# Splitting FFN weights in the DMA queue instead of on VectorE, with four more block steps

## Chip, core and metric

The kernel runs on one core of a Trainium2 chip. The metric is the device time of one execution in microseconds, median over the runs; lower is better. Engine names are those of the profile: PE is the TensorE matmul array, PEld its weight load, DVE is VectorE, ACT is ScalarE, POOL is GpSimd, SP is SyncE, which here only issues DMAs.

## What is computed

The reference is a backbone of two layers over 512 latent tokens of 1024 channels, all in float32. Layer 0 has two attention groups, layer 1 a Fourier mixing; both end in a gated convolutional feed-forward block (FFN). The FFN is the part that the change touches:

```
def conv_ffn(h, w_up, conv_w, conv_b, w_down):
    u = h @ w_up                                   # 512 x 1024 @ 1024 x 5632
    up = jnp.pad(u, ((0, 0), (1, 1), (0, 0)))
    u = up[:, :-2] * conv_w[0] + up[:, 1:-1] * conv_w[1] + up[:, 2:] * conv_w[2] + conv_b
    gate, val = jnp.split(u, 2, axis=-1)
    return (jax.nn.silu(gate) * val) @ w_down      # 512 x 2816 @ 2816 x 1024
```

## The kernel before

**A product of three.** PE multiplies in float32r, which keeps fewer bits than float32. So each operand is kept as a pair: a rounded high part h and the rest l = x - h. A product is then three matmuls (function `mm3`): L97 takes the high part of the weights with the high part of the activations, L98 the high part of the weights with the low part of the activations, L99 the low part of the weights with the high part of the activations. In the rows below the weight is called `wh` or `wl`.

**The split.** A weight comes by one DMA from SP into a buffer `raw` (three of them, `raw()` at L127 to L130). `split` at L119 then makes the pair: ACT copies `raw` into `wh` (that rounds), DVE subtracts `wh` from `raw` into `wl`. Pairs lie in five slots of 128 x 1024 elements each (`wpair`, L132: tag "wh" with 5 buffers and tag "wl" with 5). A slot is taken again once the last matmul that reads it is done.

**The FFN.** The 2816 inner channels are 22 steps of 128, fi = 0 to 21. A step multiplies h by the gate and the value columns of `w_up` (1 MB of weights), puts the result through the convolution (ACT, DVE), gates it and splits it for the down product. The steps are done in three groups of 8, 6 and 8 (`GROUPS`); after each group come eight down products, d = 0 to 7, each with its own weights `w_down` (512 KB, in the middle group 384 KB). Steps 0 to 2 run ahead in another form and are not touched.

**Plain and block steps.** A plain step has two pairs of 128 x 1024 and 2 x 8 x 3 = 48 matmuls of 128x512. A block step (`seven_products`) cuts the product into 2 x 2 blocks and does seven products instead of eight, in the order 1, 5, 2, 6, 4, 3, 7, each 4 x 3 = 12 matmuls of 128x256, 84 in all. Its weights are four pairs (`seven_weights`): "1" and "24" are blocks of `w_up` as they are; "57" and "63" are sums of blocks that DVE makes first (L986 to L989). Product 1 reads pair "1", products 5 and 7 read "57", products 6 and 3 read "63", products 2 and 4 read "24". The table `SEVEN` names the block steps: 10 in layer 0, 9 in layer 1.

**What sets the order.** Each engine works through its own list in order. The lists are laid out by a scheduler when the program is built; a wait at the head of a list holds all that stands behind it. In layer 0 the FFN also carries `gemv_jobs` (the modulation of layer 1: DMAs of `mod_r`, DVE at L388 and L391), which the program advances a piece at a time (`pump`).

Of the kernel before, what the change touches and what calls it, by code (L numbers as in the profile page):

```python
# [19 lines left out]
P = 128  # L20
# [13 lines left out]

SUMS = [5, 7]

SEVEN = [(5, 6, 8, 10, 12, 14, 15, 17, 18, 20), (8, 9, 11, 12, 14, 15, 17, 18, 20)]
NSKEW = [6, 5]
EPS = 1e-6
SCALE = P ** -0.5  # L40
# [34 lines left out]
def kernel(ctx: ExitStack, tc: tile.TileContext, a):  # L75
# [38 lines left out]
    def held(i):  # L114
        if i.ins.engine in fences:
            tc.add_manual_dep(i.ins, fences[i.ins.engine], mybir.DependencyInfo(
                mybir.DependencyClass.NoSync, mybir.DependencyReason.DATA), reason="fence")

    def split(h, l, src, eng=V):  # L119
        i = S.copy(out=h, in_=src), eng.tensor_tensor(out=l, in0=src, in1=f(h), op=ALU.subtract)  # L120
        for j in i:
            held(j)

    cp = ctx.enter_context(tc.tile_pool(name="cp", bufs=1))
    wp = ctx.enter_context(tc.tile_pool(name="wp", bufs=1))
# [825 lines left out]
    def up_weights(l, pairs, fis, eng=V):  # L951
        for fi in fis:
            r = raw([P, 2, KC, P], a["w_up"][l, fi])
            for i in range(2):
                wh, wl = pairs([P, KC, P])
                split(wh, wl, r[:, i, :, :], eng)
                yield [(wh[:, k, :], wl[:, k, :]) for k in range(KC)]
# [23 lines left out]
    def seven_weights(l, fi):  # L981
        r = raw([P, 2, KC, P], a["w_up"][l, fi])
        s = mk(wp, [P, 4, KH, P], F32, "raw", 3)
        a4 = r.rearrange("p i (c k) n -> p (i c) k n", c=2)

        for j in (V.tensor_tensor(out=s[:, 0:2], in0=a4[:, 3::-3], in1=a4[:, 2].unsqueeze(1).to_broadcast(  # L986
                      [P, 2, KH, P]), op=ALU.add),
                  V.tensor_tensor(out=s[:, 2], in0=s[:, 0], in1=a4[:, 0], op=ALU.add),
                  V.tensor_tensor(out=s[:, 3], in0=s[:, 2], in1=a4[:, 1], op=ALU.add)):  # L989
            held(j)  # L990
        w = {}
        for names, src in (("1", a4[:, 0:1]), ("57", s[:, 0:2]), ("63", s[:, 2:4]), ("24", a4[:, 1::2])):
            wh, wl = wpair([P, len(names), KH, P])
            split(wh, wl, src)
            for i, n in enumerate(names):
                w[n] = wh[:, i], wl[:, i]
        return w
# [59 lines left out]
    def ffn(l, xp, ready, pre, mid, gem, plain=None):  # L1057
# [116 lines left out]
        for gi, (f0, nch) in enumerate(GROUPS):  # L1174
            end = gi == len(GROUPS) - 1
            for fi in range(max(f0, FIRST), f0 + nch):
                if fi == SUMS[l]:
                    bs = seven_inputs(xp)
                if fi in SEVEN[l]:
                    cc = [conv(fi, i, u, None, i == 1) for i, u in enumerate(seven_products(l, fi, pps, bs))]  # L1180
                else:
                    cc = []
                    for i, w in enumerate(up_weights(l, wpair, [fi])):
                        ps = mk(pps, [P, T], F32, "mm", 6)
                        up_mm(ps, w, slice(0, T))
                        cc.append(conv(fi, i, ps))
                gated(fi, cc[0], cc[1], f0)
                if l == 0 and fi not in SEVEN[l]:
                    pump(gem, GP[0])
            g_ = [gs[fi] for fi in range(f0, f0 + nch)]  # L1190
            ws = {}

            def part(d, hs, ps=None):
                ps, sl = y_mm(pps, ws[d], g_, hs, True, ps)
                if gi == 0:
                    S.copy(out=yT[:, d, sl], in_=ps[:, sl])
                else:
                    V.tensor_tensor(out=yT[:, d, sl], in0=yT[:, d, sl], in1=ps[:, sl], op=ALU.add)
                if end:
                    ys.add(pps, yT[:, d, sl], hs)  # L1200

            def weights(d):
                r = raw([P, nch, P], a["w_down%d" % gi][l, d])
                wh, wl = (xp.spare if end and 4 <= d < 7 else wpair)([P, nch, P])
                split(wh, wl, r)
                ws[d] = [(wh[:, c, :], wl[:, c, :]) for c in range(nch)]


            hs = {d: [0, 1] if not end or d == 0 else [0] for d in range(KC)}
            begun = {}  # L1210
            if end:
                pump(gem, 100)
                fence()
            keep = dict(fences)
            fences.clear()
            for d in range(2):
                weights(d)
            fences.update(keep)
            for d in range(2):
                begun[d] = y_mm(pps, ws[d], g_, hs[d], False)[0]  # L1220
            for d in range(KC):
                if d not in ws:
                    weights(d)
                part(d, hs[d], begun.get(d))
                if gem is not None and not end:
                    pump(gem, GP[1])
            if end:
                mid(ys)
                for d in range(1, KC):
                    part(d, [1])  # L1230
# [300 lines left out]
```

## Time and profile before

| | |
|---|---|
| median of 3 runs | 1158.47 us (1157.93 to 1159.31) |
| the profiled execution | 1163.01 us, its span on the core 1161.2 us |
| PE, DVE, ACT, POOL busy | 1119.1, 860.7, 577.2, 169.1 us |
| moved by DMA | 145.31 MB, mean 125 GB/s; the main queue takes 35.1% of the 16 DMA engines' span |
| FFN of layer 0 / layer 1 | about 335 to 685 us / 780 to 1131 us of the span |

A row of the groups reads: line, engine, operation, output<-inputs, shapes, count, then busy us and mean ns of one, then the idle time ahead of them and what ended it. Rows of the timeline have start, duration, engine, line and operation. Matmuls overlap in the pipeline, so the time that one costs is the distance between two starts, not its own duration. In rows of windows the number behind each engine is its busy time in the stretch.

### The profile page before, as it was taken

The numbers are of one execution on the slowest core, as the hardware profiler recorded it, in microseconds if no ns is written. First come the engines' busy times: TensorE is split into PE (matmuls) and PEld (weight loads), VectorE is DVE, ScalarE is ACT, GpSimd is POOL, SyncE is SP. The second block draws the span as 40 slices with busy tenths as digits, with TensorE's granted clock in tenths as the row PEclk, the third lists the DMA queues.
The fourth block names the chain that finished last, engine by engine and source line by source line (L and its number), as shares of the span: only waits on it lengthen the run. The fifth ranks groups of instructions, "written<-read, shape, count | busy, mean of one in ns | idle before, by whom it ended". The sixth has DMA issues, their size and how long they took to land.

```text
span 1161.2 us, 19052 instructions
## 1 busy us (share of the span) xinstructions
PE 1119.1 (96%) x7658; PEld 965.9 (83%) x7658; DVE 860.7 (74%) x1402; ACT 577.2 (50%) x1025; POOL 169.1 (15%) x181
## 2 busy tenths in 40 slices
PE   7999999999999999999899998989999999999995
PEld 4689889669888978887798898869888888899895
DVE  5573776675679966987899658878997497579745
ACT  4342355566665634551465445556843365265442
POOL 1122433212420000000000143430000000000023
PEclk9899999999999999999999999999999999999998
DMA  9532110775202455445524400531217233223212
GB/s 371 201 123 73 37 37 1 290 267 205 74 27 85 146 183 222 175 163 179 189 86 156 145 1 19 185 124 38 73 53 274 73 109 110 76 106 109 91 56 73
DMA packets 29440, 145.31 MB, mean 125 GB/s; under 512 B 2980, under 2 KB 7716, under 8 KB 16424
## 3 DMA queue, kind: packets, MB, share of 16 engines
q1 hardware_dynamic: 29352, 144.09, 35.1%
q8 instruction: 60, 0.98, 0.3%
q14 instruction: 28, 0.23, 0.1%
HBM read 141.98 MB, written 2.10 MB: 124 GB/s over the span
## 4 chain that ended last, share of the span: by engine, by line
PE 80%; DVE 9%; ACT 4%; DMA 3%; issue 1%; POOL 1%; DVEq 0%; SPq 0%; POOLq 0%; ACTq 0%
PE mm L97 22%; PE mm L99 21%; PE mm L98 21%; PE PT L798 2%; PE gm L417 1%; DMA raw<-in_w_up 1%; DVE md_t L288 1%; ACT wh L120 1%; PE O L97 1%; DVE wl L120 1%; PE S L97 1%; PE gm L97 1%; PE O L98 1%; PE gm L98 1%; PE gm L99 1%
## 5 line engine op out<-in xcount | busy, mean ns | idle before, releaser
L120 ACT CAST wh<-raw 128x1024 fp32r<-128x1024 f32 (+2 forms) x189 | 179.9, 965 | 160.1 <-PE mm L98 70.5
L120 DVE TENSOR_TENSOR wl<-raw,wh 128x1024 fp32r<-128x1024 f32 (+3 forms) x177 | 200.4, 1140 | 73.3 <-ACT wh L120 73.1
L97 PE MATMUL mm<-hh,wh 128*128 128x256 f32 (+2 forms) x652 | 220.9, 339 | 2.4 <-ACT wh L120 1.9
L99 PE MATMUL mm<-hh,wl 128*128 128x256 f32 (+2 forms) x652 | 219.0, 336 | 0.2 <-DVE wl L120 0.2
L98 PE MATMUL mm<-hl,wh 128*128 128x256 f32 (+2 forms) x652 | 218.7, 335 | 0.0
L97 PEld LDWEIGHTS mm<-hh,wh 128*128 128x128 f32 x652 | 122.9, 188 | 19.3 <-ACT wh L120 2.3
L99 PEld LDWEIGHTS mm<-hh,wl 128*128 128x128 f32 x652 | 123.1, 189 | 14.9 <-issue 0.4
L263 POOL TENSOR_TENSOR gacc<-gacc,sq 128x256 f32<-128x256 f32 (+1 forms) x35 | 30.2, 864 | 718.4 <-ACT sq L261 717.5
L98 PEld LDWEIGHTS mm<-hl,wh 128*128 128x128 f32 x652 | 123.1, 189 | 13.7
L97 PE MATMUL mm<-xh,wh 128*128 128x512 f32 (+1 forms) x368 | 131.5, 358 | 0.2 <-ACT wh L120 0.2
L98 PE MATMUL mm<-xl,wh 128*128 128x512 f32 (+1 forms) x368 | 130.7, 355 | 0.1
L99 PE MATMUL mm<-xh,wl 128*128 128x512 f32 (+1 forms) x368 | 129.9, 354 | 0.0
L97 PE MATMUL mm<-zh,wh 128*128 128x256 f32 x304 | 87.1, 287 | 1.2 <-ACT wh L120 1.2
L99 PE MATMUL mm<-zh,wl 128*128 128x256 f32 x304 | 84.9, 279 | 0.4 <-DVE wl L120 0.4
L98 PE MATMUL mm<-zl,wh 128*128 128x256 f32 x304 | 84.9, 279 | 0.0
L97 PEld LDWEIGHTS mm<-xh,wh 128*128 128x128 f32 x368 | 69.1, 188 | 13.1 <-issue 1.6
L98 PEld LDWEIGHTS mm<-xl,wh 128*128 128x128 f32 x368 | 69.1, 188 | 11.2 <-DVE xl L120 0.3
L99 PEld LDWEIGHTS mm<-xh,wl 128*128 128x128 f32 x368 | 69.0, 188 | 10.9
L1079 ACT ACTIVATE cv<-mm,cols 128x512 f32<-128x512 f32 x64 | 49.7, 777 | 27.8 <-PE mm L99 21.6
L97 PEld LDWEIGHTS mm<-zh,wh 128*128 128x128 f32 x304 | 57.6, 189 | 5.1 <-ACT sq L1025 2.9
L99 PEld LDWEIGHTS mm<-zh,wl 128*128 128x128 f32 x304 | 57.6, 190 | 0.7 <-DVE wl L120 0.6
L391 DVE SCALAR_TENSOR_TENSOR gacc<-raw,scol,gacc 128x1024 f32<-128x1024 f32 x42 | 53.8, 1282 | 5.8 <-DMA raw<-in_mod_r 5.3
(386 smaller groups left out, 2655.0 us busy)
## 6 DMA issues: line engine op xcount, KB each, us to landing
raw<-in_w_up SPq DMA_DIRECT2D x44, 1024.0 KB, 4.9
raw<-in_mod_r SPq DMA_DIRECT2D x24, 1024.0 KB, 5.0
raw<-in_mod_p SPq DMA_DIRECT2D x16, 1024.0 KB, 4.9
raw<-in_w_down SPq DMA_DIRECT2D x32, 512.0 KB, 3.8
raw<-in_w_in SPq DMA_DIRECT2D x6, 1024.0 KB, 4.8
raw<-in_w_down SPq DMA_DIRECT2D x16, 384.0 KB, 3.1
raw<-in_w_out SPq DMA_DIRECT2D x4, 1024.0 KB, 4.9
raw<-in_w_f SPq DMA_DIRECT2D x8, 512.0 KB, 3.5
```

The lines of the kernel that those rows point to most:

```text
L97: i = PE.matmul(out, lhsT=ah, rhs=bh, start=start, stop=False, skip_group_check=skip)
L98: PE.matmul(out, lhsT=ah, rhs=bl, start=False, stop=False, skip_group_check=skip)
L99: return i, PE.matmul(out, lhsT=al, rhs=bh, start=False, stop=stop, skip_group_check=skip)
L120: i = S.copy(out=h, in_=src), eng.tensor_tensor(out=l, in0=src, in1=f(h), op=ALU.subtract)
L263: G.tensor_tensor(out=self.acc[:, sl], in0=self.acc[:, sl], in1=sq[:, sl], op=ALU.add)
L288: m = V.scalar_tensor_tensor(out=t, in0=yT[:, k, hs], scalar=der[:, l, gi, k:k + 1], in1=R, op0=ALU.mult, op1=ALU.mult)
L391: held(V.scalar_tensor_tensor(out=acc, in0=w[:, i, :], scalar=scol[:, 0, k:k + 1], in1=acc, op0=ALU.mult, op1=ALU.add))
L417: PE.matmul(ps[32 * q:32 * q + 32, :], lhsT=spad[:, k, :], rhs=w[:, q * T:(q + 1) * T], start=k == 0, stop=k == KC - 1)
L798: PE.transpose(out=pt[:, j * P:(j + 1) * P], in_=Ps[j][:, off:off + P], identity=ident)
L1079: S.activation(out=cv, in_=ps, func=AF.Identity, bias=bc, scale=wc[1])
```

## The change

The new helper `split_in` makes a pair without `raw` and without DVE. A DMA from POOL casts the weight from HBM into `wh`; ACT writes -`wh` into `wl`; a second DMA from POOL reads the same weight from HBM again and adds it onto `wl`, which leaves the weight minus its rounded part. Plain steps from fi = 3 on and the down products of the first two groups use it in place of `raw` and `split`. Block steps use it for "1" and "24"; they still load the whole of `w_up` into `raw` by SP for the sums, and "57" and "63" are still split by ACT and DVE. The down products of the last group are as before. `SEVEN` has 12 and 11 steps, 23 instead of 19. The modulation pieces are pumped once or twice in turn per down product. POOL's descriptor ring is twice as large.

```
-SEVEN = [(5, 6, 8, 10, 12, 14, 15, 17, 18, 20), (8, 9, 11, 12, 14, 15, 17, 18, 20)]
+SEVEN = [(5, 6, 8, 9, 10, 12, 14, 15, 16, 18, 19, 20), (8, 9, 10, 11, 12, 14, 15, 16, 18, 19, 20)]
...
+    def split_in(h, l, src):
+        G.dma_start(out=h, in_=src)
+        held(S.activation(out=l, in_=f(h), func=AF.Copy, scale=-1.0))
+        G.dma_start(out=l, in_=src, accum_op=ALU.add)
...
         w = {}
-        for names, src in (("1", a4[:, 0:1]), ("57", s[:, 0:2]), ("63", s[:, 2:4]), ("24", a4[:, 1::2])):
+        for names, src, way in (("1", a["w_up"][l, fi, :, 0:1, :KH], split_in), ("57", s[:, 0:2], split),
+                                ("63", s[:, 2:4], split), ("24", a["w_up"][l, fi, :, :, KH:], split_in)):
             wh, wl = wpair([P, len(names), KH, P])
-            split(wh, wl, src)
+            way(wh, wl, src)
...
                     cc = []
-                    for i, w in enumerate(up_weights(l, wpair, [fi])):
+                    for i in range(2):
+                        wh, wl = wpair([P, KC, P])
+                        split_in(wh, wl, a["w_up"][l, fi, :, i])
                         ps = mk(pps, [P, T], F32, "mm", 6)
-                        up_mm(ps, w, slice(0, T))
+                        up_mm(ps, [(wh[:, k, :], wl[:, k, :]) for k in range(KC)], slice(0, T))
                         cc.append(conv(fi, i, ps))
...
             def weights(d):
-                r = raw([P, nch, P], a["w_down%d" % gi][l, d])
                 wh, wl = (xp.spare if end and 4 <= d < 7 else wpair)([P, nch, P])
-                split(wh, wl, r)
+                src = a["w_down%d" % gi][l, d]
+                if end:
+                    split(wh, wl, raw([P, nch, P], src))
+                else:
+                    split_in(wh, wl, src)
...
-                    pump(gem, GP[1])
+                    pump(gem, GP[1] + d % 2)
...
-    nc = bacc.Bacc("TRN2", target_bir_lowering=False, num_devices=1, dynamic_dma_scratch_size=1024)
+    nc = bacc.Bacc("TRN2", target_bir_lowering=False, num_devices=1, dynamic_dma_scratch_size=2048)
```

In the changed kernel the lines from L120 on stand 6 to 18 lines lower; the two DMAs of `split_in` are L126 (cast) and L128 (add), its ACT copy is L127.

Two places show what the built lists hold. The first is POOL's list at layer 1's first block steps, fi = 8 to 10. Before, POOL has nothing to do in the FFN of layer 1 up to its last group; its list goes from the end of the Fourier stage straight to the sums of squares at the end:

```order
L120 TENSOR_TENSOR wl_1241_8128<-raw_1239_8125,wh_1240_8127 128x1024
L120 TENSOR_TENSOR wl_1243_8132<-raw_1239_8125,wh_1242_8131 128x1024
L263 TENSOR_TENSOR acc_1171_7741<-acc_1171_7741,sq_1208_7967 128x512
L263 TENSOR_TENSOR gacc_1658_11260<-gacc_1658_11260,sq_1659_11266 128x256
L263 TENSOR_TENSOR gacc_1658_11260<-gacc_1658_11260,sq_1664_11301 128x256
```

In the changed kernel there stands between them, among others (128x512 is pair "1", 128x2x512 is pair "24"):

```order
L126 DMA wh_1413_9716<-in_w_up 128x512
L128 DMA wl_1414_9717<-in_w_up 128x512
L126 DMA wh_1419_9729<-in_w_up 128x2x512
L126 DMA wh_1429_9846<-in_w_up 128x512
L128 DMA wl_1420_9730<-in_w_up 128x2x512
L128 DMA wl_1430_9847<-in_w_up 128x512
L126 DMA wh_1435_9859<-in_w_up 128x2x512
L126 DMA wh_1447_9978<-in_w_up 128x512
```

Per block step POOL now issues four DMAs. The cast into `wh_1435` ("24" of step 10) waits for the slot of `wh_1417` ("63" of step 9), that is, for the last matmul of product 3 of step 9; "24" of step 9 (`wh_1419`) waits for product 3 of step 8 in the same way.

The second place is PE's list in the middle of a block step, where pair "24" comes in. Before (step 9; `wh_1437` is "57", `wh_1439` is "63", `wh_1441` is "24"):

```order
L99 MATMUL mm_1443_9618<-zh_1359_9094,wl_1438_9607 128x256
L97 MATMUL mm_1444_9619<-zh_1361_9098,wh_1439_9610 128x256
L98 MATMUL mm_1444_9619<-zl_1362_9099,wh_1439_9610 128x256
L99 MATMUL mm_1444_9619<-zh_1361_9098,wl_1440_9611 128x256
...
L97 MATMUL mm_1443_9618<-hh_5_66,wh_1441_9614 128x256
L98 MATMUL mm_1443_9618<-hl_6_67,wh_1441_9614 128x256
L99 MATMUL mm_1443_9618<-hh_5_66,wl_1442_9615 128x256
```

In the changed kernel (step 9 again; `wh_1415` is "57", `wh_1417` is "63", `wh_1419` is "24"; `wh_1429` and `wh_1431` are "1" and "57" of step 10):

```order
L99 MATMUL mm_1421_9734<-zh_1346_9214,wl_1416_9722 128x256
L97 MATMUL mm_1438_9865<-hh_5_66,wh_1429_9846 128x256
L98 MATMUL mm_1438_9865<-hl_6_67,wh_1429_9846 128x256
L97 MATMUL mm_1437_9864<-zh_1346_9214,wh_1431_9851 128x256
L98 MATMUL mm_1437_9864<-zl_1347_9215,wh_1431_9851 128x256
L97 MATMUL mm_1422_9735<-zh_1348_9218,wh_1417_9725 128x256
...
L97 MATMUL mm_1422_9735<-zh_1350_9222,wh_1419_9729 128x256
L98 MATMUL mm_1422_9735<-zl_1351_9223,wh_1419_9729 128x256
L99 MATMUL mm_1437_9864<-zh_1346_9214,wl_1432_9852 128x256
L99 MATMUL mm_1421_9734<-hh_5_66,wl_1420_9730 128x256
```

Five matmuls of the next step (the four with `wh_1429` and `wh_1431`, and `wl_1432`) now stand inside this one, ahead of the first matmul that reads `wl_1420`. From that matmul to the last one that reads `wh_1417` (the end of product 3, which frees the slot for "24" of step 10) there are 31 matmuls of 128x256, both counted; between them stands no product that doesn't need "24" or come behind it in the list.

## The prediction

> **What bounds the kernel now.** I read the busy times first, then the chain of work that ended last, both on the page.
>
> ```profile
> span 1161.2 us, 19052 instructions
> PE 1119.1 (96%) x7658; PEld 965.9 (83%) x7658; DVE 860.7 (74%) x1402; ACT 577.2 (50%) x1025; POOL 169.1 (15%) x181
> PE 80%; DVE 9%; ACT 4%; DMA 3%; issue 1%; POOL 1%; DVEq 0%; SPq 0%; POOLq 0%; ACTq 0%
> ```
>
> PE sets the time, so an edit is worth what it does to PE's list. The next question is whether PE ever waits in the FFN, which is all that the change touches. The windows answer it (stretch, its length, busy us of PE, PEld, DVE, ACT and POOL with counts, granted clock, DMA share, GB/s): the FFN of layer 0, that of layer 1, and two pieces of layer 0 in which DMA share is high.
>
> ```profile
> 335.00:685.00 350.00, 344.95 (x2127) 300.99 (x2126) 286.31 (x361) 171.91 (x261) 11.71 (x13) 1.00 0.42 146
> 780.00:1131.00 351.00, 350.55 (x2183) 305.62 (x2182) 268.20 (x396) 183.66 (x295) 5.07 (x6) 1.00 0.29 97
> 540.00:560.00 20.00, 18.35 (x85) 13.80 (x83) 13.75 (x16) 3.15 (x5) 0.00 (x0) 1.00 0.76 263
> 560.00:580.00 20.00, 18.16 (x135) 17.55 (x136) 18.29 (x22) 12.76 (x20) 0.00 (x0) 0.91 0.44 163
> ```
>
> PE idles 5.05 us of 350 in layer 0, of which 1.65 + 1.84 = 3.5 us lie in the two short pieces, and 0.45 us of 351 in layer 1. DVE is busy 286 and 268 us there. So a lighter DVE can win about 5 us in all, while a wait on PE costs its whole length.
>
> **What a step takes.** In layer 1 the timeline of PE gives the starts of a plain step (939.35 to 950.54, 11.19 us) and of the two block steps behind it (950.54 to 971.21, 20.67 us, so 10.34 each):
>
> ```profile
> 939.00 0.28 PE L97 MATMUL mm<-zh,wh 128*128 128x256 f32 x1
> 939.12 0.28 PE L98 MATMUL mm<-zl,wh 128*128 128x256 f32 x1
> 939.23 0.28 PE L99 MATMUL mm<-zh,wl 128*128 128x256 f32 x1
> 939.35 0.40 PE L97 MATMUL mm<-hh,wh 128*128 128x512 f32 x1
> ...
> 950.54 0.28 PE L97 MATMUL mm<-hh,wh 128*128 128x256 f32 x1
> ...
> 971.21 0.40 PE L97 MATMUL mm<-hh,wh 128*128 128x512 f32 x1
> ```
>
> A 128x256 matmul costs (939.35 - 939.00) / 3 = 0.117 us from start to start. A plain step more as a block step gains 11.19 - 10.34 = 0.85 us; four of them gain 3.4 us.
>
> **The new chain.** What a pair needed before, and its nearest relations in time:
>
> ```profile
> L120 ACT CAST wh<-raw 128x1024 fp32r<-128x1024 f32 x143 | 147.9, 1050 | 95.9 <-PE mm L98 48.0 <-DMA raw<-in_w_down 19.0 <-PE mm L99 14.0
> L120 DVE TENSOR_TENSOR wl<-raw,wh 128x1024 fp32r<-128x1024 f32 x141 | 171.2, 1221 | 63.3 <-ACT wh L120 63.2
> ```
>
> ```profile
> raw<-in_w_down SPq DMA_DIRECT2D x32, 512.0 KB, 3.8
> ...
> raw<-in_w_f SPq DMA_DIRECT2D x8, 512.0 KB, 3.5
> ...
> out_xT<-xT SPq DMA_DIRECT2D x8, 256.0 KB, 2.1
> ```
>
> Before, the DMA lands in `raw` ahead of need, so from the moment a slot of the five pairs is free only ACT (1.05 us) and DVE (1.22 us) lie between it and a usable pair: 2.3 us. Now both DMAs write into the slot itself. They can't start until the slot is free, and they run one after the other with ACT between: cast, negate, add. Call that chain C.
>
> Where that matters is the loop shown in the second place above. "24" of step 10 takes the slot that "63" of step 9 leaves. From PE's first matmul on `wl` of "24" to the last on `wh` of "63" there are 31 matmuls: 30 x 0.117 + 0.28 = 3.79 us. Then the chain C runs, and only then can PE start the first `wl` matmul of "24" of the next step; the list lets nothing else past. A round of this loop takes C + 3.79 us; a block step without it takes 10.34 us. **C may last 6.55 us; all above it is a stall, once per transition between two consecutive block steps.**
>
> C has five terms. Cast: the trace has no casting DMA; the nearest row is the plain one of 512 KB, 3.8 us from issue to landing. ACT: 1.05 us. Add: reads the weight and the destination; I take 3.8 us and a second stream of 524,288 bytes. What the 16 engines move when busy follows from the third window: 263 GB/s at a share of 0.76, so 346 GB/s, hence 1.5 us more: 5.3 us. [...]
>
> ```profile
> L686 POOL TENSOR_SCALAR K<-K,krs 128x128 f32<-128x128 f32 x12 | 6.2, 540 | 1.8 <-DVE krs L157 1.8
> ```
> ```profile
> L120 POOL TENSOR_TENSOR wl<-raw,wh 128x512 fp32r<-128x512 f32 x10 | 13.1, 1328 | 48.6 <-ACT wh L120 48.6
> ```
>
> I take 0.54 us each. C = 0.54 + 3.8 + 1.05 + 0.54 + 5.3 = 11.2 us, and the stall is 4.7 us.
>
> Bounds: from below no issue time and both DMAs like the fastest 512 KB row, C = 3.5 + 1.05 + 3.5 = 8.05, stall 1.5 us. From above 1.33 us for an issue and the add twice a plain DMA, C = 1.33 + 3.8 + 1.05 + 1.33 + 7.6 = 15.1, stall 8.6 us.
>
> [...]
>
> **The sum.** Consecutive steps within one group of `SEVEN`, counted in the table: layer 0 has 5-6, 8-9, 9-10, 14-15, 15-16, 18-19, 19-20, layer 1 8-9, 9-10, 10-11, 11-12, 14-15, 15-16, 18-19, 19-20: 15 transitions x 4.7 = **+70 us**.
>
> Twelve places more have a block step on one side alone. Behind a block step that ends a run (8 times) the next plain pair takes the slot of "63" or "24", with the same late release, and its DMAs stand in POOL's list behind those already waiting. At 4 further places a block step opens a group and its pairs take slots that the last down products leave. There the next PE work is longer or the slot a little earlier; I take half a stall, 2.3 us, bounds 0 and half of the upper stall: 12 x 2.3 = **+28 us**. Where a block step follows a plain one inside a group (4 times) the slot comes free half a plain step (5.6 us) earlier, which covers C: 0.
>
> Plain steps and down products otherwise: the slot is taken four pairs ahead, and a pair is 24 matmuls of 128x512, half of 11.19 us, so 22 us of PE work hide 11 us of chain: 0. In the middle group a pair has three quarters of that, 4 x 4.2 = 17 us: 0. If the add took twice what I take, C would be 16.5 us, and even the middle group would just be covered.
>
> DVE loses the subtraction of those pairs and ACT keeps one copy for each. That buys what PE waited for DVE and late weights in the two short pieces of layer 0, which their load of 263 GB/s had made: **-3.5 us**. The remaining 1.5 us of idle are left as they are. The modulation pieces move by one product on DVE, which has 64 us free in that stretch: 0. SP issues fewer large loads and waits for `raw` less: 0, nobody waits for it in time. The larger descriptor ring: 0.
>
> Sum: 70 + 28 - 3.4 - 3.5 = +91 us. The span of 1161.2 becomes 1252; the profiled execution was 1163.0 and the median is 2.7 us below the span, so **1250 us**. Bounds: 15 x 1.5 - 6.9 = +16, 1174 us; 15 x 8.6 + 12 x 4.3 - 3.4 = +177, 1335 us.
>
> **Rivals.** *Faster: the chain fits.* If both DMAs take 2.75 us or less and their issue hides, C is within 6.55 us, PE never waits, and the gains stay: 1158.5 - 3.4 - 5.05 = 1150 us. For it speaks the 256 KB store, 2.1 us; with 0.76 us more for a second 256 KB at 346 GB/s that is 2.9 us, close. Against it: 32 loads of 512 KB have a median of 3.8 us, and POOL has to issue in order. Chance 0.09. Between the two, a chain of about 6.8 us would eat just the gains: no change, 0.02.
>
> *The DMA engines become the bound.* A block step moves 1.05 MB into `raw`, 0.79 MB by cast and 0.79 MB by add. At 346 GB/s that is 7.6 us, and 9.9 us if an added byte costs twice: within 10.34. If it costs four times, a plain step needs (1.05 + 4.2) MB / 346 GB/s = 15.2 us against 11.19, the down products 7.6 against 5.6 and 5.7 against 4.2. The remaining 15 plain steps from step 3 on, and 16 products of each kind, add 60 + 32 + 24 us; the chain is then 0.54 + 3.8 + 1.05 + 0.54 + 3.8 + 3 x 1.5 = 14.3 us, stall 7.7: 15 x 7.7 + 12 x 3.9 = 162. Together with the gain of 3.4 about 1433 us. For it: each pair is now read twice from HBM, in 23 x 4 + 15 x 4 + 32 x 2 = 216 DMAs that POOL issues. Against it: only 0.42 and 0.29 of the DMA engines' time is used in the two layers now. Chance 0.07.
>
> **How the numbers follow.** The forecast holds 0.82, its own range is that of its bounds, 1174 to 1335 us, and I state 1172 to 1340 with what runs differ by. Left out are the chain that fits, no change and the bandwidth bound, 0.18. Faster by over 0.2% (about the least that can be told here): 0.09; within: 0.02; slower: 0.89.
>
> **What the changed profile would show.** Right: PE waits ahead of L99 matmuls for the adding DMA of L128, about once per consecutive block step, each some 2 to 8 us; the distance from one block step to the next grows from 10.3 to about 15 us at layer 1's steps 8 to 12; plain steps keep 11.2 us; PE's share falls below 92%; DVE's busy time falls by over 100 us with no gain from it; in the DMA issues, L126 and L128 take 3.5 us or more for 512 KB. The half stalls are right if a few us of waiting stand at the first pair behind each run of block steps. Wrong: if PE's waits for L128 are near zero, the chain fits in 6.55 us; if plain steps and down products stretch too, with DMA share near 1, it is the engines and not the slot; if L97 waits and not L99, the cast is what is late.

## The result

The changed kernel takes 1366.93 us (median of 4 runs, 1364.31 to 1370.23) against 1158.2 us (1156.82 to 1159.31): a ratio of 1.1804, with a 95% interval from 1.1775 to 1.1834. The direction is the one forecast, the size is not: 209 us were lost where 91 us were expected, and the time lies above the stated 1340 us.

Time and queues on the page of the changed kernel (queue rows: packets, MB, share of the 16 engines' span):

```profile
span 1366.0 us, 19728 instructions
PE 1183.6 (87%) x7802; PEld 1023.8 (75%) x7802; DVE 782.5 (57%) x1322; ACT 587.3 (43%) x1049; POOL 334.8 (25%) x397
...
q0 software_dynamic: 36992, 97.01, 32.2%
q1 hardware_dynamic: 22584, 113.68, 22.9%
```

The span grew by 204.8 us. PE is idle for 1366.0 - 1183.6 = 182.4 us instead of 42.1, which is 140 us of it. The other 64.5 us are PE's busy time, although four more block steps ought to have shortened it by 3.4 us: the same matmuls ran slower, at a mean granted clock of 0.925 against 0.986. DVE got 78 us lighter, and no gain from that can be seen.

The waits (who waited for whom, us in all, times, longest) show what PE stands for:

```profile
POOL wl L128 <- ACT wl L127: 340.7, 77, 34.4
POOL wh L126 <- PE mm L99: 234.5, 66, 12.5
...
PE mm L99 <- DMA wl<-in_w_up: 60.7, 24, 5.8
...
PE mm L97 <- DMA wh<-in_w_up: 33.5, 11, 5.8
```

PE waits for an adding DMA (L99) and, in the same steps, for a cast (L97: pair "1" of the next step, whose cast stands in POOL's list behind the cast of "24"). POOL in its turn waits for PE's last L99 matmul on the old pair. That is the loop of the prediction. In layer 1, steps 8 to 12, POOL's timeline gives its period (L126 is a cast, L128 an add; the first row of each kind belongs to "24", the second to "1"):

```profile
1046.40 0.73 POOL L126 DMA_DIRECT2D wh<-in_w_up  x1 [4.41 <-PE mm L99]
1047.80 0.57 POOL L126 DMA_DIRECT2D wh<-in_w_up  x1 [0.66 <-PE mm L99]
1052.46 1.10 POOL L128 DMA_DIRECT2D wl<-in_w_up  x1 [4.09 <-ACT sq L1027]
1053.99 0.91 POOL L128 DMA_DIRECT2D wl<-in_w_up  x1 [0.43 <-DVE cv L1089]
1066.89 0.73 POOL L126 DMA_DIRECT2D wh<-in_w_up  x1 [12.00 <-PE mm L99]
```

And PE's timeline has the matmul that waited for the add, and those behind it:

```profile
1061.23 0.58 PE L99 MATMUL mm<-hh,wl 128*128 128x256 f32 x1 [3.56 <-DMA wl<-in_w_up]
1061.62 0.42 PE L97 MATMUL mm<-hh,wh 128*128 128x256 f32 x1
1061.83 0.41 PE L98 MATMUL mm<-hl,wh 128*128 128x256 f32 x1
...
1064.33 0.28 PE L97 MATMUL mm<-zh,wh 128*128 128x256 f32 x1
1064.45 0.28 PE L98 MATMUL mm<-zl,wh 128*128 128x256 f32 x1
```

From the cast's issue at 1046.40 to the L99 matmul at 1061.23 the chain took 14.8 us. In the next three steps, read in the same way, it took 11.6, 12.8 and 12.2 us: 12.85 us on average, where 11.2 were predicted and 6.55 could be hidden. The second half of the loop, from that matmul to the next cast, was to take 3.79 us and takes 5.66, 7.36 and 5.97 us. The matmuls above show why: right behind the stall they start 0.21 us apart, from 1064.3 on 0.12. Of the 2.54 us that the second half is longer on average, the slow matmuls are 2.0; the rest is the 0.4 us from the end of the last matmul on `wh` of "63" to the cast, and two more matmuls in steps 10 and 11, where PE's timeline has 33 in place of the 31 of step 9. The windows have the granted clock (the number behind POOL) for this stretch, for the rest of the way to the cast, and for the next whole step:

```profile
1061.23:1064.18 2.95, 2.94 (x14) 2.95 (x15) 0.00 (x0) 0.00 (x0) 0.00 (x0) 0.50 0.17 31
1064.18:1066.89 2.71, 2.71 (x24) 2.71 (x24) 0.64 (x1) 1.05 (x1) 0.00 (x0) 0.99 0.00 0
```
```profile
1072.61:1091.81 19.20, 14.26 (x85) 13.61 (x85) 9.91 (x13) 6.65 (x12) 3.29 (x4) 0.73 0.55 138
```

In this step PE runs at a granted clock of 0.50 for 2.95 us after the stall; in the next one it does so from 1078.51 to 1084.65, 6.1 us. A block step takes 19 to 20 us instead of 10.34. The same holds for the other runs of block steps: at 14 of the 15 transitions PE waits for the add, and these waits follow each other at 17.3 to 22.4 us, 19.4 on average.

Where the 205 us lie, stage by stage (from the first matmul of a stage to the first of the next, in PE's timeline, in us; the kernels on the right are explained below):

| stage | before | after | onlyblock | blockraw | order24 | chainpool |
|---|---|---|---|---|---|---|
| layer 0, steps 3 to 7 | 53.5 | 71.4 | 71.3 | 64.5 | 68.2 | 74.3 |
| layer 0, first down products | 46.7 | 52.2 | 52.9 | 52.6 | 60.8 | 46.7 |
| layer 0, steps 8 to 13 | 64.5 | 100.8 | 94.0 | 77.1 | 81.6 | 101.6 |
| layer 0, second down products | 37.9 | 42.6 | 42.0 | 50.3 | 58.6 | 36.0 |
| layer 0, steps 14 to 21 | 89.4 | 128.1 | 118.9 | 90.8 | 102.3 | 141.0 |
| from the end of layer 0's third down products to the end of layer 1's first | 219.1 | 233.8 | 219.5 | 233.5 | 234.1 | 220.5 |
| layer 1, steps 8 to 13 | 63.8 | 101.0 | 97.5 | 70.5 | 78.7 | 104.6 |
| layer 1, second down products | 33.6 | 38.3 | 33.6 | 37.7 | 39.5 | 33.6 |
| layer 1, steps 14 to 21 | 85.2 | 134.6 | 124.6 | 92.9 | 109.5 | 133.4 |

The five groups that hold block steps lose 179 us. The down products and the plain steps of layer 1, which were costed at nothing, lose 5.5 + 4.7 + 14.7 + 4.7 = 30 us.

### The profile page after: what moved, and what is told of

Read it like the earlier page. It is cut to its first block, busy times and chain, and to the rows that moved or that the text cites. A ratio compares the mean times of both kernels' runs of the same rounds, so it can differ in the third digit from the quotient of the medians.

```text
span 1366.0 us, 19728 instructions
## 1 busy us (share of the span) xinstructions
PE 1183.6 (87%) x7802; PEld 1023.8 (75%) x7802; DVE 782.5 (57%) x1322; ACT 587.3 (43%) x1049; POOL 334.8 (25%) x397
## 3 DMA queue, kind: packets, MB, share of 16 engines
q0 software_dynamic: 36992, 97.01, 32.2%
## 4 chain that ended last, share of the span: by engine, by line
PE 42%; issue 35%; POOL 9%; DMA 7%; DVE 6%; ACT 2%; POOLq 0%; DVEq 0%; SPq 0%; ACTq 0%
PE mm L99 10%; PE mm L97 9%; PE mm L98 9%; DMA wl<-in_w_up 5%; POOL wl L128 4%; POOL wh L126 4%; PE PT L804 1%; PE gm L423 1%; PE O L97 1%; PE S L97 1%; PE gm L97 1%; PE O L98 1%; PE S L99 1%; PE gm L98 1%; PE gm L99 1%
## 5 line engine op out<-in xcount | busy, mean ns | idle before, releaser
L99 PE MATMUL mm<-hh,wl 128*128 128x256 f32 (+2 forms) x636 | 221.3, 350 | 60.7 <-DMA wl<-in_w_up 60.7
L97 PE MATMUL mm<-hh,wh 128*128 128x256 f32 (+2 forms) x636 | 223.3, 351 | 48.6 <-DMA wh<-in_w_up 33.5
L120 DVE TENSOR_TENSOR wl<-raw,wh 128x1024 fp32r<-128x1024 f32 x77 | 95.2, 1240 | 183.6 <-ACT wh L120 183.5
L127 ACT ACTIVATE wl<-wh 128x1024 fp32r<-128x1024 f32 (+2 forms) x108 | 100.5, 936 | 212.1 <-DMA wh<-in_w_up 104.6
L99 PEld LDWEIGHTS mm<-hh,wl 128*128 128x128 f32 x636 | 131.5, 207 | 80.2 <-DMA wl<-in_w_up 69.3
L97 PEld LDWEIGHTS mm<-hh,wh 128*128 128x128 f32 x636 | 133.1, 209 | 64.4 <-issue 26.0
L120 ACT CAST wh<-raw 128x1024 fp32r<-128x1024 f32 (+1 forms) x89 | 88.0, 998 | 146.2 <-PE mm L98 100.3
L97 PE MATMUL mm<-xh,wh 128*128 128x512 f32 (+1 forms) x368 | 135.1, 367 | 8.4 <-ACT xh L120 8.4
L128 POOL DMA_DIRECT2D wl<-in_w_up x76 | 71.4, 947 | 278.3 <-ACT wl L127 216.5
L99 PE MATMUL mm<-xh,wl 128*128 128x512 f32 (+1 forms) x368 | 133.2, 362 | 1.1 <-DMA wl<-in_w_down 1.0
L97 PE MATMUL mm<-zh,wh 128*128 128x256 f32 x368 | 117.0, 318 | 12.8 <-ACT sq L1027 6.2
L99 PE MATMUL mm<-zh,wl 128*128 128x256 f32 x368 | 113.3, 308 | 0.5 <-DVE wl L120 0.5
L98 PE MATMUL mm<-zl,wh 128*128 128x256 f32 x368 | 113.4, 309 | 0.0
L126 POOL DMA_DIRECT2D wh<-in_w_up x76 | 50.7, 673 | 223.1 <-PE mm L99 223.1
L97 PEld LDWEIGHTS mm<-zh,wh 128*128 128x128 f32 x368 | 81.0, 220 | 18.2 <-ACT sq L1027 8.0
L97 PEld LDWEIGHTS mm<-xh,wh 128*128 128x128 f32 x368 | 71.2, 193 | 22.5 <-ACT xh L120 9.7
L99 PEld LDWEIGHTS mm<-zh,wl 128*128 128x128 f32 x368 | 80.9, 220 | 1.0 <-DVE wl L120 0.9
L98 PEld LDWEIGHTS mm<-zl,wh 128*128 128x128 f32 x368 | 81.5, 222 | 0.0
L98 PEld LDWEIGHTS mm<-xl,wh 128*128 128x128 f32 x368 | 70.9, 193 | 12.9 <-DVE xl L120 1.7
```

The costliest lines, as they stand in the source:

```text
L97: i = PE.matmul(out, lhsT=ah, rhs=bh, start=start, stop=False, skip_group_check=skip)
L98: PE.matmul(out, lhsT=ah, rhs=bl, start=False, stop=False, skip_group_check=skip)
L99: return i, PE.matmul(out, lhsT=al, rhs=bh, start=False, stop=stop, skip_group_check=skip)
L126: G.dma_start(out=h, in_=src)
L127: held(S.activation(out=l, in_=f(h), func=AF.Copy, scale=-1.0))
L128: G.dma_start(out=l, in_=src, accum_op=ALU.add)
```

## Experiments on the block steps

The theory: pair "24" can't be started before product 3 of the step before has left its slot; the chain cast, negate, add is longer than what is left, and PE waits. The rivals: the load that POOL's DMAs put on the DMA engines, and the block steps themselves.

**The slot order (order24).** The edit:

```
-        for names, src, way in (("1", ...), ("57", ...), ("63", ...), ("24", ...)):
+        for names, src, way in (("1", ...), ("24", ...), ("57", ...), ("63", ...)):
```

> The changed kernel with one tuple reordered: the pairs of a block step are taken in the order 1, 24, 57, 63 instead of 1, 57, 63, 24. All DMAs and their bytes stay. Pair 24 of step j then takes the slot that pair 1 of step j-1 left after its first product, eight products of 12 matmuls (8 x 12 x 0.117 = 11.2 us) ahead of its use, in place of the slot of 63, whose release leaves 31 matmuls. Slot theory: the chain measured in layer 1 (11.6 to 14.8 us from the cast's issue to the first L99 matmul) is then covered but for 0.4 to 3.6 us a step; consecutive block steps go from about 19.7 us back to 10.7 to 14, and the time falls by 85 us or more, to 1285 or below. PE's granted clock recovers with it, to 0.95 or more, although the traffic is the same. Rival, load on the DMA engines or HBM (same 97 MB by POOL): no change, 1355 to 1375, clock about 0.925.

Measured: 1302.41 us, 1.1245 of before (1.1216 to 1.1274), 64 us less than the changed kernel with the same DMAs. The block groups' loss falls from 179 to 84 us, as the theory wants; its bound of 1285 us was missed, since the down products got worse by 26 us (the table). The page and the waits:

```profile
PE 1149.1 (89%) x7802; PEld 993.4 (77%) x7802; DVE 781.1 (60%) x1322; ACT 590.6 (46%) x1049; POOL 334.6 (26%) x397
```
```profile
PE misc L409 <- ACT gacc L405: 27.0, 3, 10.6
...
PE mm L97 <- ACT sq L1033: 24.3, 14, 5.5
```

PE's busy time falls with its waits, from 1183.6 to 1149.1 us, at the same traffic. The largest waits that are left end with ACT, whose list also holds the negations. That the negations cause them is not shown for this kernel.

**Block steps alone, plain and down pairs alone (onlyblock, blockraw).** The first gives plain steps and down products back to `raw` and `split`, the second the pairs of the block steps:

```
-                        split_in(wh, wl, a["w_up"][l, fi, :, i])
+                    for i, w in enumerate(up_weights(l, wpair, [fi])):
...
-                if end:
-                    split(wh, wl, raw([P, nch, P], src))
-                else:
-                    split_in(wh, wl, src)
+                split(wh, wl, raw([P, nch, P], src))
```
```
-        for names, src, way in (("1", a["w_up"][l, fi, :, 0:1, :KH], split_in), ... ("24", ..., split_in)):
+        for names, src, way in (("1", a4[:, 0:1], split), ... ("24", a4[:, 1::2], split)):
```

> The changed kernel with plain steps and down products split from raw by ACT and DVE as before; only pairs 1 and 24 of the block steps still come by casting and adding DMAs. POOL's DMAs fall from 216 to 92. Slot theory: the loss sits in the block steps and stays, 1320 to 1365 us. Load theory: POOL moves 36 MB instead of 97, its DMAs land faster, and the loss falls at least by half, to 1260 or below.

> The changed kernel with pairs 1 and 24 split from raw again; plain steps and down products keep the casting and adding DMAs (124 of them). Slot theory: these pairs have four pairs of PE work (17 to 22 us) as cover for a chain of 12 to 15 us, so almost all of the loss goes: 1150 to 1180 us; PE waits for POOL's DMAs under 15 us in all. Load theory: 61 of the 97 MB by POOL stay, and so does the larger part of the loss, 1250 us or above.

Measured: onlyblock 1322.67 us, ratio 1.1396 (1.1360 to 1.1433); blockraw 1239.16 us, ratio 1.0689 (1.0663 to 1.0715). The block steps alone make 164 us of loss with 36 MB by POOL instead of 97, so the load as a whole is not it; the load within a block step stayed the same here, and the next experiment settles that. But plain and down pairs alone cost 80 us, where 20 at most were expected (1180 us): here the theory was incomplete (next section). The two add up to more than the 209 us of the whole.

**The same wait without any new DMA (chainpool, pool2, pool1).** These start from the kernel before with 23 block steps; only the low part of "24" is written by POOL, by four, two or one subtractions:

```
-            split(wh, wl, src)
+            split(wh, wl, src, G if names == "24" else V)
+            if names == "24":
+                for _ in range(3):      # pool2: range(1); pool1: without the loop
+                    G.tensor_tensor(out=wl, in0=src, in1=f(wh), op=ALU.subtract)
```

> The kernel before with 23 block steps, and no casting or adding DMA at all. Only the low part of pair 24 is written by POOL, and four times over (the same subtraction repeated), so that from the slot's release to a usable pair it takes 1.05 + 4 x 2.87 = 12.5 us, about the chain measured in the changed kernel (11.6 to 14.8 us). DMA traffic is that of before, ACT waits for no new DMA. Slot theory: the late pair alone makes the loss; 15 transitions x (12.5 - 6.55) = 89 us at full clock, and with the matmuls slowed behind each stall (0.213 instead of 0.117 us apart for some 3 us, measured in the changed kernel) up to 135 us: 1245 to 1300 us, granted clock 0.93 to 0.96. Rival, the POOL DMAs' load on the engines, HBM or the clock is the cause: 1160 to 1170 us, clock 0.985.

> As chainpool, but the subtraction done twice instead of four times: 1.05 + 2 x 2.87 = 6.8 us, just above the 6.55 us. Slot theory: a stall of a few tenths of a us at most of the 15 transitions, 1157 to 1175 us; between one (3.9 us) and four (12.5 us, 1356 us) the loss starts at about two. Rival, a loss that grows evenly with POOL's work: a third of chainpool's loss, 1215 to 1235 us.

> The kernel before with 23 block steps and the low part of pair 24 written by POOL, once: from release to a usable pair 1.05 + 2.87 = 3.9 us, below the 6.55 us that the slot leaves. Slot theory: no stall; DVE has 1.2 us less to do in each block step, so the waits for DVE that before23 showed in its run of steps 8 to 12 (0.86 and 1.99 us) go: 1152 to 1161 us. Rival, POOL beside DVE slows DVE (its subtraction took 1446 ns instead of 1221 in chainpool): 1162 to 1175 us.

Measured: chainpool 1355.87 us, ratio 1.1672 (1.1630 to 1.1713); pool2 1217.9 us, ratio 1.0498 (1.0457 to 1.0538); pool1 1175.01 us, ratio 1.0130 (1.0103 to 1.0158). Waits, timeline and a window of chainpool:

```profile
PE mm L99 <- POOL wl L997: 123.4, 23, 8.6
...
PE mm L99 <- DVE wl L120: 11.0, 9, 4.0
```
```profile
1050.98 0.58 PE L99 MATMUL mm<-hh,wl 128*128 128x256 f32 x1 [5.20 <-POOL wl L997]
...
1070.68 0.58 PE L99 MATMUL mm<-hh,wl 128*128 128x256 f32 x1 [7.62 <-POOL wl L997]
```
```profile
1058.82 3.02 POOL L120 TENSOR_TENSOR wl<-raw,wh 128x1024 fp32r<-128x1024 f32 x1 [7.90 <-ACT wh L120]
1061.92 8.71 POOL L997 TENSOR_TENSOR wl<-raw,wh 128x1024 fp32r<-128x1024 f32 x3
```
```profile
1050.98:1053.90 2.92, 2.92 (x13) 2.92 (x14) 2.23 (x3) 0.00 (x0) 0.00 (x0) 0.50 0.59 219
```

This is the main reading of the study. One pair that is late by a chain of 12.9 us (ACT's 1.05 and POOL's 11.8), with the DMAs of the kernel before, makes 196 us of loss, nearly that of the changed kernel: the period of 19.7 us, the half clock behind the stalls (0.50 for 2.92 us behind 5.20 us of waiting), a mean clock of 0.919 (0.925 in the changed kernel). It went above the 1300 us expected: 15 transitions at 19.7 - 10.34 us make 140 us, and the expectation left out the places with a block step on one side alone. POOL's extra work slows DVE here too (the sums of L986 take 2048 ns instead of 1219), but PE waits 11.0 us for DVE's pairs against 123.4 us for POOL's. pool2 missed too: 1157 to 1175 us were expected and 1218 came. In its trace the chain is 8.5 us instead of 6.8 (ACT does two copies back to back, POOL's subtractions take 3.1 to 3.2 us), and a round of the loop takes 14.2 us; this fits the same loop with a longer chain, though no sharp threshold at 6.55 us was seen, and the time by itself lies in the range of the rival (a loss that grows evenly with POOL's work, 1215 to 1235 us). Against an even growth stands the row of all four: none, one, two and four subtractions lose 5, 15, 58 and 196 us. pool1, with 1152 to 1161 us expected, missed as well and met its rival (1162 to 1175 us).

**The table alone, and DVE's share (before23, pool1_both).** before23 changes only the table `SEVEN` of the kernel before; pool1_both also writes the low part of "1" on POOL.

> The kernel before with nothing changed but the table: 23 block steps instead of 19, all split by ACT and DVE. Slot theory: ACT and DVE need 2.3 us from the slot's release, below 6.55, so consecutive block steps run at 10.3 us and the time falls by 4 x 0.85 = 3.4 us, to 1152 to 1158. Rival, consecutive block steps are slow of themselves (DVE's sums, ACT's copies, four steps more): slower than 1160.

> As pool1, with pair 1 split by POOL too (1.33 us more on POOL, 0.69 us less on DVE per block step). Slot theory: pair 1 takes a slot freed a whole step ahead, so no stall: 1150 to 1161 us, the best of the kernels run if DVE is what holds runs of block steps. Rival, POOL beside DVE slows DVE: 1162 to 1180 us.

Measured: before23 1164.49 us, ratio 1.0046 (1.0027 to 1.0066); pool1_both 1183.57 us, ratio 1.0201 (1.0167 to 1.0234). So the four further block steps win nothing even without the new split; PE waits 9.3 us for DVE in before23:

```profile
PE mm L99 <- DVE wl L120: 9.3, 7, 2.0
```

In the kernel before that wait is 3.3 us. Relieving DVE in runs of block steps is thus a sound aim, but POOL does not serve it here: by the ratios pool1 is 10 us slower than before23 and pool1_both, above both of its expected ranges, 18. In pool1 PE's wait for DVE did fall, to 3.9 us, but it waits 11.0 us for ACT's copies at L1022, and beside POOL's subtractions DVE's own sums get slower. That the slower sums are what delays ACT is not shown. The groups of before23, then of pool1:

```profile
L986 DVE TENSOR_TENSOR raw<-raw 128x1024 f32<-128x1024 f32 x23 | 28.1, 1221 | 9.1 <-DMA raw<-in_w_up 9.0
```
```profile
L986 DVE TENSOR_TENSOR raw<-raw 128x1024 f32<-128x1024 f32 x23 | 40.5, 1761 | 14.9 <-DMA raw<-in_w_up 11.1 <-POOL wl L120 3.6
```

No kernel of this study is faster than the one before.

## Experiments on the price of a DMA and on plain and down pairs

**The path alone (poolplain).** The kernel before, with the plain loads of the down weights issued by POOL instead of SP:

```
-                r = raw([P, nch, P], a["w_down%d" % gi][l, d])
+                r = raw([P, nch, P], a["w_down%d" % gi][l, d], G)
```

> The kernel before with the down weights' plain loads into raw issued by POOL instead of SP: no cast, no add. It prices the path alone. If POOL's path is what makes a 512 KB DMA take 6 to 6.7 us to land (3.8 us from SP), these land in 5.5 to 6.5 us; if it is the casting and adding, in 3.8 to 4.5 us. The loads are prefetched, so the time moves by less than 10 us.

Measured: 1158.49 us, ratio 0.9996 (0.9973 to 1.0019). The DMA issues of poolplain, and those of the changed kernel (KB each, median us to landing):

```profile
q0 software_dynamic: 5888, 23.07, 6.2%
...
raw<-in_w_down POOLq DMA_DIRECT2D x32, 512.0 KB, 4.0
```
```profile
wh<-in_w_up POOLq DMA_DIRECT2D x53, 512.0 KB, 6.1
wl<-in_w_up POOLq DMA_DIRECT2D x53, 512.0 KB, 6.7
...
raw<-in_w_down SPq DMA_DIRECT2D x16, 512.0 KB, 4.6
...
wh<-in_w_up POOLq DMA_DIRECT2D x23, 256.0 KB, 5.7
wl<-in_w_up POOLq DMA_DIRECT2D x23, 256.0 KB, 4.9
```

A plain 512 KB load lands in 4.0 us from POOL, against 3.8 from SP: the path is not the price. Casting and adding DMAs take 6.1 and 6.7 us in the changed kernel. A part of that is the load they run under: there a plain load from SP takes 4.6 us too, and in onlyblock, with 36 MB by POOL, cast and add of 512 KB land in 4.9 and 5.7 us, still above 4.0. In engine time, POOL's 97.01 MB took 0.322 x 1366.0 = 440 us of the 16 engines, 220 GB/s, where its plain 23.07 MB took 0.062 x 1155.5 = 72 us, 322 GB/s (1155.5 us is the span of poolplain). Half the bytes hardly land sooner: 256 KB took 5.7 and 4.9 us in the changed kernel.

**Negation on POOL (blockraw_negpool, order24_negpool).** To take the negation off ACT:

```
-        held(S.activation(out=l, in_=f(h), func=AF.Copy, scale=-1.0))
+        G.tensor_scalar(out=l, in0=f(h), scalar1=-1.0, scalar2=None, op0=ALU.mult)
```

> The kernel of blockraw (1239 us) with the negation of plain and down pairs moved from ACT to POOL. ACT then waits for no cast; the chain of a pair grows by 2.87 - 1.05 = 1.8 us and keeps POOL 2.9 us longer. Theory that ACT's list is blocked: ACT stood 114.7 us at L127 for casts of down weights in blockraw and PE waited for the copies behind; most of the 80 us go, 1165 to 1200 us. Rival, the pairs themselves come too late (casts behind adds in POOL's list): the longer chain makes it no faster, 1235 to 1275 us.

> The kernel of order24 (1302 us) with all negations on POOL. Theory that ACT's list is blocked (260 us of waiting at L127 for casts in order24, and PE behind it): 1220 to 1270 us. Rival, late pairs: the chain is 1.8 us longer in each of 23 block steps and POOL holds other casts back, 1300 to 1350 us.

Measured: 1293.64 us, ratio 1.1132 (1.1086 to 1.1179), and 1399.36 us, ratio 1.2058 (1.2020 to 1.2096): 54 and 97 us worse than without, beyond even the rival's range. So moving the negation costs far more than ACT wins by it; the longer chain and the fuller POOL list were not taken apart.

**Where it starts (onlydown).** The kernel of blockraw with the plain steps split from `raw` too, as in onlyblock's edit.

> The kernel before with 23 block steps and only the down products of the first two groups by casting and adding DMAs (64 DMAs by POOL); everything else split from raw. blockraw (plain and down pairs) cost 80 us, of which about 37 stand in the down products: 1190 to 1215 us if the two add up; below 1180 if plain steps start the trouble.

Measured: 1205.96 us, ratio 1.0381 (1.0353 to 1.0409), as expected if the two add up: the down products alone cost 45 us, the plain steps the other 33. PE's waits in onlydown:

```profile
PE mm L97 <- ACT xh L120: 12.3, 4, 7.9
...
PE misc L409 <- ACT gacc L405: 9.3, 3, 5.0
PE mm L99 <- DMA wl<-in_w_down: 9.1, 5, 5.8
```

**ACT's list and POOL's list (actfree, ahead, and both).** In actfree ACT negates a tile that is always there; POOL waits for the cast by a one-column read ahead of the add. The low part of these weights is then not the weight minus its rounded part; this kernel, actfree_ahead, actfree_ahead1 and after_actfree leave that out and show times alone:

```
-        held(S.activation(out=l, in_=f(h), func=AF.Copy, scale=-1.0))
-        G.dma_start(out=l, in_=src, accum_op=ALU.add)
+        held(S.activation(out=l, in_=f(hl)[:, :l.shape[1], :P], func=AF.Copy, scale=-1.0))
+        seen = G.tensor_scalar(out=tiny, in0=f(h)[:, 0, :1], scalar1=-1.0, scalar2=None, op0=ALU.mult)
+        follow(G.dma_start(out=l, in_=src, accum_op=ALU.add), seen)
```

In ahead the casts of down products are issued earlier, and the add is made to stand behind them in POOL's list (`follow`); ahead1 does that for one pair instead of two, and in plain steps it puts both casts of a step ahead of its adds (the edit in short):

```
-                    split_in(wh, wl, src)
+                    begin(d + 1)                      # the cast of the next pair (ahead: of the next two)
+                    add = split_in(wh, wl, src, False)   # negate and add alone
+                    follow(add, casts[max(casts)])
```

> The kernel of blockraw (1239 us) with one difference: in POOL's list the casts of down products stand one to two pairs ahead of the adds (cast of d+1 and d+2 before add of d), where in blockraw they mostly alternate, so that the next cast can't be issued before the add of the pair before it, which waits for that pair's cast and negation. ACT's work and all bytes stay. Theory that POOL's list serialises the pairs (a pair every 7 to 10 us there, where PE needs one every 4.2 to 5.6 us): the down products get 20 us or more of their 37 us back, 1200 to 1220 us in all. Rival, ACT's list held by L127, or the DMA engines: no change, 1230 to 1245 us.

> The kernel of blockraw (1239 us) with ACT taken out of the chain: ACT writes the negative of another tile that has long been there into wl, so it waits for the slot alone and never for a cast; the adding DMA still waits for the cast, by a one-column read on POOL. The low part of these weights is thereby not the right one; times, bytes, POOL's order of DMAs stay. Theory that ACT's list held at L127 delays its copies behind (L1086, L1205, L405), for which DVE and PE wait: half or more of the 80 us go, 1165 to 1200 us. Rival, late pairs or DMA load: at most the 1.05 us of the negation per chain, 1222 to 1245 us.

> The same with the casts ahead of the adds as in the kernel of ahead (1230 us); low parts again not the right ones. If the two mechanisms make up the cost of plain and down pairs: 1160 to 1180 us. If DMA landing times (6 to 7.5 us) remain: 1195 us or above.

Measured: ahead 1229.99 us, ratio 1.0599 (1.0553 to 1.0645); actfree 1234.47 us, ratio 1.0651 (1.0604 to 1.0698); actfree_ahead 1238.74 us, ratio 1.0667 (1.0624 to 1.0711). All three within 10 us of blockraw, none as a single cause would have it. POOL's timeline in actfree, in layer 1's first down products, shows what remains (`tiny` is the read that waits for the cast):

```profile
914.29 0.88 POOL L126 DMA_DIRECT2D wh<-in_w_down  x1
920.95 0.37 POOL L128 TENSOR_SCALAR tiny<-wh 128x1 f32<-128x1 f32 x1 [5.78 <-DMA wh<-in_w_down]
921.53 0.90 POOL L129 DMA_DIRECT2D wl<-in_w_down  x1 [0.21 <-issue]
922.13 0.88 POOL L126 DMA_DIRECT2D wh<-in_w_down  x1
```

Cast, wait for it, add, and only then the next cast: 7.84 us a pair, where PE uses one up in 5.6. In these rows the pairs are late not by their slots but by POOL's list. With the casts two ahead (actfree_ahead) the list jams elsewhere:

```profile
952.50 0.55 POOL L1223 DMA_DIRECT2D wh<-in_w_down  x1 [8.66 <-PE mm L99]
953.07 0.25 POOL L129 TENSOR_SCALAR tiny<-wh 128x1 f32<-128x1 f32 x1
953.25 0.96 POOL L130 DMA_DIRECT2D wl<-in_w_down  x1
```

The early cast waits 8.66 us for its slot, and the add of the pair that PE needs first stands behind it. So the casts were put exactly one pair ahead:

> The kernel of actfree (1234 us; low parts of these weights not the right ones) with each cast exactly one pair ahead of the add before it in POOL's list. In actfree's trace POOL alternates, cast (6.1 to 6.7 us to land), add, next cast, and a down product of layer 1 comes every 7.4 to 7.9 us where PE needs 5.6; in actfree_ahead the casts stood two ahead and waited 8.9 us for their slot with the adds behind them. One ahead, two casts are under way at a time and none waits for a slot: a pair every 4 us, and layer 1's first down products go from 57 to about 47 us, all in all 1190 to 1215 us. Rival, the casting DMAs have no more throughput than one per 7 us: two under way land later, 1230 to 1245 us.

> The kernel of blockraw (1239 us) with each cast one pair ahead of the add before it, the negation on ACT. If POOL's order and ACT's wait are separate costs, between actfree_ahead1 and blockraw: 1200 to 1225 us; if POOL's order is the whole, the same as actfree_ahead1; if landing, 1230 to 1245 us.

Measured: actfree_ahead1 1219.91 us, ratio 1.0536 (1.0493 to 1.0579); ahead1 1227.37 us, ratio 1.0607 (1.0560 to 1.0654). The first ends 5 us above the range expected, the second between two of the ranges: part of the cost lies elsewhere. In the down products it is clear. The four groups of them (layer 1's first counted without the plain steps before it) take 161 us in before23's trace, 202 in blockraw, 186 in actfree, 183 in ahead1 and 172 in actfree_ahead1: POOL's order and ACT's wait are worth 16 to 20 us each, and together 31 of the 41. POOL's timeline in actfree_ahead1, same place:

```profile
908.51 0.58 POOL L1223 DMA_DIRECT2D wh<-in_w_down  x1 [0.27 <-issue]
909.15 0.87 POOL L130 DMA_DIRECT2D wl<-in_w_down  x1
914.18 0.22 POOL L129 TENSOR_SCALAR tiny<-wh 128x1 f32<-128x1 f32 x1 [4.16 <-DMA wh<-in_w_down]
914.62 0.60 POOL L1223 DMA_DIRECT2D wh<-in_w_down  x1 [0.22 <-issue]
```

A pair every 6.1 us, near PE's 5.6. The rest of the loss in these kernels stands in the groups with plain steps. Against before23 they lose 34 us in blockraw, but 39 in ahead1 and 47 in actfree_ahead1, although both put the casts of a plain step ahead of its adds, and 50 in actfree. So neither POOL's order within a plain step nor ACT's wait shows as the cause there, and it stays open.

**How much of the whole is ACT's list (after_actfree).** The changed kernel with actfree's edit everywhere:

> The changed kernel (1367 us) with ACT out of the chain in the same way, block steps too; low parts not the right ones. Slot theory: in the block steps the chain loses the negation and ACT's queue, about 1.05 + 0.5 us at 15 transitions, and plain and down pairs gain what actfree gains: 1290 to 1340 us, PE's waits for the adding DMA stay. Theory that ACT's list is the whole of it: below 1250 us.

Measured: 1365.33 us, ratio 1.1779 (1.1735 to 1.1824): no change from 1366.93. Both theories were off. The stages explain it: the five block groups win 14.6 us, as one microsecond at 15 transitions would, and the stretch before layer 1's first down products loses 13. In the block steps ACT's list is thus worth about 1 us per transition, the size of the negation itself (1.06 us).

## Why the prediction was right and wrong

The step that failed is the price of a round of the loop, C + 3.79 us, with matmuls that go on at full clock behind a stall; and plain steps and down products stood at nothing.

- **The loop through the slot of "63", right.** PE waits at L99 for the adding DMA at 14 of the 15 transitions between block steps; chainpool makes nearly the same loss without those DMAs, and another slot order removes 95 us of it from the block groups. Not named was the second wait of each round, 2.4 to 2.8 us at L97 in layer 1's steps 8 to 12, for the cast of the next step's "1", issued behind that of "24"; it lies within the chain's time, so the wait at L99 is shorter, 1.6 to 3.6 us.
- **The chain, mis-sized by 1.65 us.** 12.85 us instead of 11.2, in layer 1's steps 8 to 12. From the start of its issue to the negation a cast took 4.3 to 5.3 us, 4.7 on average (taken: 0.54 + 3.8). The 0.54 us taken for an issue was the author's estimate, from the time of a small operation of POOL; no run shows it for these DMAs: POOL took 0.73 to 0.74 us to issue a cast of "24" and 1.08 to 1.10 us to issue its add. From the negation's end to the add's issue 0.45 to 0.47 us pass each time, which no term held. From the add's issue to PE's matmul there are 5.8 to 6.0 us three times, about the 0.54 + 5.3 taken, and 8.8 once. Worth 15 x 1.65 = 25 us.
- **The second half of the loop, the larger miss.** Its 31 matmuls were priced at the 0.117 us of a PE that never stops; it takes 6.33 us on average, not 3.79. A stall was taken to cost its length, and behind the stalls PE ran at half clock for 3 to 6 us besides, 2.0 of the 2.54 us. Worth 15 x 2.54 = 38 us here; through all stalls PE's busy time grew by 64.5 us. The granted clock was 0.50 for 2.95 us behind 3.56 us of waiting, for 6.1 us behind 1.91 us and for 2.94 us behind 1.63 us, and 1.00 behind 1.74 us: the length of the wait alone does not tell which. The prediction left this term out.
- **The twelve other places, too small.** The block groups lose 179 us. With 15 x (19.41 - 10.34) = 136 us at the transitions (19.41 us is the mean from cast to cast) 43 us are left for these places and the gain of four more block steps together, where 28 - 3.4 were taken: 19 us more. What one place costs was not taken apart.
- **Plain steps and down products at nothing, wrong.** "The slot is taken four pairs ahead" counted the slot and not POOL's list, in which the next cast stands behind the add of the pair before. They lose 30 us in the changed kernel and 80 where they are alone. For the down products POOL's order and ACT's wait are shown as the cause of 31 of the 41 us in blockraw; for the plain steps the cause stays open.
- **The 3.4 us of four more block steps, and 3.5 us from DVE, not seen.** before23 shows no gain: in runs of block steps PE waits for DVE, 9.3 us in all there. DVE's busy time fell by 78 us and not by over 100.
- **The rivals.** The chain that fits is excluded by its 12.85 us. The DMA engines are excluded as the main cause in the block steps by chainpool and order24; but casting and adding do take 1.65 times the engine time per byte of the plain loads by SP (220 against 363 GB/s, the latter from the q1 row), for which only that rival had a term.

The misses add up: 25 + 38 + 19 + 30 + 3.5 = 115 us, where the stages of the table lose 209 us and 91 were forecast, 118 us more. That it comes out so close is in part luck, since chain and second half are means of four and three rounds in one place.

## What to carry to other kernels

Before a buffer's filling is made longer, find the last reader that frees it and the first that needs it again, and compare the time between with the whole chain in between; prefetching through a staging buffer is what kept that chain at 2.3 us here (ACT 1.05 us, DVE 1.22 us). Count an issuing queue as a resource in its own right: two dependent DMAs per tile in one queue's order gave a pair every 7.84 us here, and one every 6.1 us with the casts one pair ahead, while the slots were free. And price a stall of PE by its length plus the slow matmuls behind it, 2.0 us a round on average in layer 1's steps 8 to 12.

## What was not expected of the hardware

- Behind PE's longer waits its granted clock was 0.50 for some microseconds, in layer 1's steps 8 to 12 behind each wait of 2.40 to 2.77 us for a cast: right behind it at 1091.81 and 1112.15, and at 1052.96 and 1072.61 from 1.2 and 1.9 us after the wait's end on. Behind the waits for the add that came 4.6 to 8.3 us after the casts' it was 0.50 for another 2.95 us (wait of 3.56 us, matmuls 0.213 instead of 0.117 us apart), 6.1 us (1.91 us, at 1078.51) and 2.94 us (1.63 us), but 1.00 behind one of 1.74 us at 1116.79, and also behind a single one of 1.99 us in before23. What decides between them is not shown.
- A casting or adding DMA of 512 KB took 6.1 and 6.7 us to land in the changed kernel and 4.9 and 5.7 in onlyblock, where a plain one from the same queue took 4.0 in poolplain. In the changed kernel 256 KB took 5.7 and 4.9 us.
- Beside POOL's subtractions a DVE sum of 128x1024 took 1761 ns in pool1, where it took 1221 in before23.
